# A hybrid decoder block: the last two v tiles made as a pair, round trips issued by two engines, another order at the seams

## The chip, the cores and the metric

The kernel runs on one core of one Trainium2 chip. The metric is the time of one execution on the device in microseconds (us), the median of several runs.

## What is computed

One decoder block on 512 tokens of width 2048 in float32. A modulated RMS norm feeds one input projection; its columns go to two mixers, an RWKV-7 group of 16 heads of 64 (1024 columns each of r, k and v, and small ones for decay, `a` and gate) and a pooling group. Their outputs, 2048 rows, go through an output projection, and a gated MLP with a causal convolution follows.

```python
h = _rmsnorm(x, norm1_g[l]) * (1.0 + sc1) + sh1
p = h @ w_in[l]
y_rwkv = _rwkv7_mixer(p[..., :N_RWKV_COLS], mu_shift[l], w0[l], w2[l], a0[l], a2[l],
                      g2[l], k_k[l], k_a[l], r_k[l], ln_x_w[l], ln_x_b[l])
y_pool = _pool_mixer(p[..., N_RWKV_COLS:], pool_w[l], pool_b[l], pool_scale[l])
mix = jnp.concatenate([y_rwkv, y_pool], axis=-1) @ w_out[l]
x = x + gt1 * mix
h = _rmsnorm(x, norm2_g[l]) * (1.0 + sc2) + sh2
x = x + gt2 * _conv_ffn(h, w_up[l], conv_w[l], conv_b[l], w_down[l])
```

Inside the RWKV mixer every column is first mixed with that of the token before (the token shift), and each head carries a 64x64 state from token to token:

```python
sa = jnp.einsum('bhvk,bhk->bhv', S, a_t)
S = S * w_t[:, :, None, :] + sa[..., None] * b_t[:, :, None, :] + v_t[..., None] * k_t[:, :, None, :]
y = jnp.einsum('bhvk,bhk->bhv', S, r_t)
```

## The kernel before

**Products in three passes.** Each float32 product of a weight tile is made of three matmuls (`mm3`, lines 128 to 130: hi weights by hi activations, hi by lo, lo by hi). `split_weights` loads 128x512 weights into `wraw` (four buffers), ScalarE (ACT) casts the hi part `whi` (L122) and VectorE (DVE) subtracts to get `wlo` (L124). One tile of the input projection, 128 columns by 512 tokens, is 16 k-blocks of 128, that is 48 matmuls of 128x512 and four weight loads. Activations are split in the same way: `split_act` makes `ah` (L151, ACT) and `al` (L152, DVE) from a row of 128 channels.

**Stages.** First the norm and the first tiles of the projection (to about 204 us in the trace), then the mixer stage, four quads of four heads (g = 0 to 3), then the output projection, then the MLP, which takes most of the time. In the mixer stage the small matmuls of the quads, 64x64 or 64x128, stand between tiles of the input projection that make the columns of the next quad: `win_some` makes tiles and writes each, shifted by `shift` (L268 on ACT, L269 on DVE), to DRAM (`spill` to `sp`), and `load_cells` brings them back into the cells R, K and V. For each quad two tiles of k, two of r and two of v are made.

**A quad.** `front` makes the gates: the decay from `sg` (a sigmoid, L423), its running sum, `ep` and the second `sg` (exponentials, L443 and L444), `al` (a sigmoid, L428), and the normaliser `inv` (L451 squares, L452 the sum of them on TensorE, L456 a logarithm, L457 an exponential). Sigmoid, tanh, exponentials and logarithm need tables on ACT, and a load of one shows as ACT_TABLE_LOAD; `preload_act_table_set` (L430) asks for the table with logarithm and exponential early. `rest` does the remainder: `scores` (matmuls L485, masked into `sb` by DVE at L487), tokens in rows by `by_token` (matmuls L497, copied by ACT at L500 into tokTB and tokTV), the same for k (L534, copied at L536 into tokTK), the second scores (L545, masked into `sk` at L547), and a sum over heads (L554).

**The round trips.** A triangular system of 16x16 blocks is solved in another layout. `sb` goes to DRAM in eight transfers (`dn`, L510), comes back as `nl` (L512) once all eight have landed, DVE copies it (L560) and works through 28 small steps (L567, L569) to `xyl`; this goes to DRAM as `dxy` (L573) and comes back into X in eight transfers (L577). PE then multiplies X with the identity (L583) and goes on: L593, the mask into `pm` (L596), L603 and L609, the addition into X (L605), L593 again. All the transfers are issued by SyncE (SP).

**Mixer rows.** The finished rows `rs` of quads 0 to 2 go to DRAM (`mixd`, L706), as do those of the pools (L339). Behind the last quad's front, fourteen rows are read back (`mxl`, L775, in the four `wraw` buffers), split and multiplied by the output weights (`wout`); the last quad's two rows (`last_mix`) are split directly and are used later.

**What sets the order.** The program is written stage by stage; a scheduler places instructions on each engine by their priority (`tc.high_priority`), and each engine then runs its own list in that order. `ada_rest` spreads 96 products for later modulation (`war`, loaded from `ada` at L382, DVE at L383) over spots behind given instructions. PSUM buffers for small products (`bt`) are handed on when the reader of an earlier one is done.

Of the kernel before, what the change touches and what calls it, by code (L numbers as in the profile page):

```python
# [18 lines left out]
P = 128  # L19
# [8 lines left out]
NQ = 4  # L28
# [36 lines left out]
def block_kernel(ctx, tc, a, out, stop=None, dbg=None):  # L65
# [121 lines left out]
    if True:  # L187
# [78 lines left out]
        if True:  # L266
# [13 lines left out]
            xwa = ra.tile([P, T], F32, tag="xwa", name="xwa")  # L280
            shift(pf[0], 24, xwa)
            xg = two(cell("X", "xg"))
            RKV = ("R", "K", "V")
            rkv0 = [cell(RKV[i], "rkv"[i]) for i in range(3)]
            for i in range(2):
                shift(pf[1 + i], 25 + i, xg[:, i, :])
            for i, (t, x, m) in enumerate(((0, 0, 0), (1, 0, 8), (2, 0, 16), (0, 1, 1), (1, 1, 9))):
                shift(pf[3 + i], m, two(rkv0[t])[:, x, :])
                if i == 0:
                    S.activation(xwa[0:64, :], xwa[0:64, :], AF.Tanh)  # L290
            ps0ctx.close()
# [4 lines left out]
            def sigmoids():  # L296
                for i in range(2):
                    S.activation(xg[:, i, :], xg[:, i, :], AF.Sigmoid)
                    S.copy(xgh[i], xg[:, i, :])
                V.tensor_tensor(xg1l, xg[:, 0, :], xg1h[:, :].bitcast(F32), op=ALU.subtract)  # L300
                V.tensor_tensor(xg2[64:96, :], xg[64:96, 1, :], xg2[64:96, :].bitcast(F32), op=ALU.subtract)

            sigmoids()

# [100 lines left out]
    def front(g, rkv):  # L405
# [21 lines left out]
        for x in range(2):  # L427
            act = S.activation(two(al)[:, x, :], psal[:, x, :], AF.Sigmoid, bias=c2("a0", x))  # L428
        with tc.issue_after(act.ins):
            act = S.preload_act_table_set("natural_log_exp_and_others")  # L430
# [33 lines left out]
    def rest(g, rkv, fr):  # L464
# [42 lines left out]
        for s in range(2):  # L507
            for i in range(4):
                o = 64 * s + 16 * i
                nc.sync.dma_start(dn[s, i].rearrange("j i t -> i j t"), nts[o : o + 16, :, 0, 16 * i : 16 * i + 16])  # L510
        nl = ra.tile([P, 16, 16], F32, tag="nl", name="nl")
# [62 lines left out]
        for s in range(2):  # L574
            for i in range(4):
                o = 64 * s + 16 * i
                nc.sync.dma_start(rows(X)[o : o + 16, :, 16 * i : 16 * i + 16],  # L577
                                  dxy[o : o + 16].rearrange("j a t -> a j t"))
# [125 lines left out]
        for x in range(2):  # L704
            if g < NQ - 1:
                nc.sync.dma_start(mixd[2 * g + x], two(rs)[:, x, :])  # L706
            else:
                last_mix.append(split_act(NM + x, two(rs)[:, x, :]))

    sp, last_mix = {}, []  # L710

    def win_some(pairs, which):
# [12 lines left out]
    def load_cells(g, names):  # L725
# [6 lines left out]
        return got  # L732

    UNDER = {0: POOLS[0:1], 1: POOLS[1:2], 2: POOLS[2:4]}
    rkv = rkv0
    with hp():
        fr, norm = front(0, rkv)
    for g in range(NQ):
        pairs = (2 * g + 2, 2 * g + 3)
# [8 lines left out]
        if g < NQ - 1:  # L748
            win_some(pairs, (0, 2))
            with tc.high_priority(offset=50000):  # L750
# [6 lines left out]
        with hp():  # L757
            next(quad, None)
            if g < NQ - 1:
                rkv = [r, k] + load_cells(g + 1, (2,))  # L760
        if g < NQ - 1:
            ada_rest(24 * g, 24 * g + 24)
# [7 lines left out]

    M = []

    def load_mix(i):
        t = wp.tile([P, WC], F32, tag="wraw", name="mxl", bufs=4)
        nc.sync.dma_start(t, mixd[MIX_ORDER[i]])  # L775
        M.append(split_act(i, t))

    for i in range(NM):
        load_mix(i)
    part = []  # L780
# [499 lines left out]
```

## Time and profile before

| what | value |
|---|---|
| median of 3 runs | 2308.88 us (2304.35 to 2310.61) |
| the profiled execution | 2309.01 us, span 2307.2 us |
| TensorE busy | 2197.2 us, 95% |
| VectorE busy | 1509.7 us, 65% |
| ScalarE busy | 926.7 us, 40% |
| mean granted TensorE clock | 0.985 of full speed |

The span is what the profile covers, from the first to the last instruction; the time of the execution has 1.8 us more around it. PE is TensorE's matmuls, DVE VectorE, ACT ScalarE, POOL GpSimd and SP SyncE. A line such as L497 is a line of the kernel, shown above. Where a row has brackets, they give the idle time of the engine just ahead of it and what ended this.

### The profile page before, as it was taken

The numbers are of one execution on the slowest core, as the hardware profiler recorded it, in microseconds if no ns is written. First come the engines' busy times: TensorE is split into PE (matmuls) and PEld (weight loads), VectorE is DVE, ScalarE is ACT, GpSimd is POOL, SyncE is SP. The second block draws the span as 40 slices with busy tenths as digits, with TensorE's granted clock in tenths as the row PEclk, the third lists the DMA queues.
The fourth block names the chain that finished last, engine by engine and source line by source line (L and its number), as shares of the span: only waits on it lengthen the run. The fifth ranks groups of instructions, "written<-read, shape, count | busy, mean of one in ns | idle before, by whom it ended". The sixth has DMA issues, their size and how long they took to land.

```text
span 2307.2 us, 41832 instructions
## 1 busy us (share of the span) xinstructions
PE 2197.2 (95%) x16306; PEld 1874.6 (81%) x16306; DVE 1509.7 (65%) x2536; ACT 926.7 (40%) x1551; POOL 408.0 (18%) x390
## 2 busy tenths in 40 slices
PE   7999898889889999999999999999999999999997
PEld 5786666576667799799999999999999788888886
DVE  7896777686866569866665666656666445464457
ACT  4335242433523355534444444444444333343333
POOL 0000000000000016644334343433432000000000
PEclk9999999999999999999999999999999999999999
DMA  9885656566665575433333333333333766666555
GB/s 355 296 316 164 182 189 193 179 224 200 199 220 173 186 236 172 127 115 119 110 112 117 119 115 111 118 110 109 121 114 118 244 191 211 194 195 202 166 160 179
DMA packets 198041, 401.41 MB, mean 174 GB/s; under 512 B 37585, under 2 KB 50641, under 8 KB 193617
## 3 DMA queue, kind: packets, MB, share of 16 engines
q1 hardware_dynamic: 197842, 398.73, 54.0%
q8 instruction: 128, 2.10, 0.4%
q14 instruction: 71, 0.58, 0.1%
HBM read 364.56 MB, written 34.09 MB: 173 GB/s over the span
## 4 chain that ended last, share of the span: by engine, by line
PE 54%; DMA 1%; DVE 1%; ACT 0%; issue 0%; SPq 0%; DVEq 0%; ACTq 0%
PE b L128 18%; PE b L129 18%; PE b L130 18%; DMA wraw<-wdn 1%; DVE x L1102 0%; DMA ald<-actd 0%; DMA x<-x2d 0%; DVE wlo L124 0%; ACT whi L122 0%; DVE x L831 0%; DVE al L152 0%; PE b L178 0%; ACT ah L151 0%; DVE acc L827 0%; DVE sl L997 0%
## 5 line engine op out<-in xcount | busy, mean ns | idle before, releaser
L122 ACT CAST whi<-wraw 128x512 fp32r<-128x512 f32 (+1 forms) x594 | 361.4, 610 | 847.2 <-DMA wraw<-wup 263.0
L124 DVE TENSOR_TENSOR wlo<-wraw,whi 128x512 fp32r<-128x512 f32 (+1 forms) x578 | 407.3, 708 | 292.3 <-ACT whi L122 285.2
L128 PE MATMUL b<-ah,whi 128*128 128x512 f32 (+1 forms) x980 | 350.0, 357 | 8.1 <-ACT whi L122 7.1
L130 PE MATMUL b<-ah,wlo 128*128 128x512 f32 (+1 forms) x980 | 349.3, 357 | 3.5 <-DVE wlo L124 3.2
L129 PE MATMUL b<-al,whi 128*128 128x512 f32 (+1 forms) x980 | 348.3, 355 | 0.0
L130 PE MATMUL b<-hh,wlo 128*128 128x512 f32 (+1 forms) x640 | 236.6, 370 | 5.2 <-DVE wlo L124 5.2
L128 PE MATMUL b<-hh,whi 128*128 128x512 f32 (+1 forms) x640 | 237.1, 371 | 0.3 <-ACT whi L122 0.3
L129 PE MATMUL b<-hl,whi 128*128 128x512 f32 (+1 forms) x640 | 236.6, 370 | 0.0
L128 PEld LDWEIGHTS b<-ah,whi 128*128 128x128 f32 x980 | 185.8, 190 | 36.6 <-ACT whi L122 10.9
L130 PEld LDWEIGHTS b<-ah,wlo 128*128 128x128 f32 x980 | 185.7, 189 | 32.9 <-DVE wlo L124 6.1
L129 PEld LDWEIGHTS b<-al,whi 128*128 128x128 f32 x980 | 186.0, 190 | 25.7
L997 DVE TENSOR_TENSOR pl<-raw,ph 128x768 fp32r<-128x768 f32 x104 | 102.0, 980 | 154.0 <-ACT ph L996 154.0
L128 PE MATMUL mm<-ah,whi 128*128 128x512 f32 x444 | 183.2, 413 | 6.1 <-ACT whi L122 6.0
L130 PE MATMUL mm<-ah,wlo 128*128 128x512 f32 x444 | 181.0, 408 | 4.4 <-DVE wlo L124 4.4
L129 PE MATMUL mm<-al,whi 128*128 128x512 f32 x444 | 184.0, 414 | 0.0
L985 POOL TENSOR_TENSOR sums<-sums,raw 128x256 f32<-128x256 f32 x104 | 107.2, 1030 | 420.7 <-DVE sl L997 414.8
L130 PE MATMUL b<-tk,sl 128*128 128x256 f32 x624 | 176.7, 283 | 0.5 <-DVE sl L997 0.5
L129 PE MATMUL b<-tk,sh 128*128 128x256 f32 x624 | 176.6, 283 | 0.0
L128 PE MATMUL b<-tk,sh 128*128 128x256 f32 x624 | 176.0, 282 | 0.0
L996 ACT CAST ph<-raw 128x768 fp32r<-128x768 f32 x104 | 86.4, 830 | 167.7 <-PE b L129 160.5
L984 POOL TENSOR_TENSOR sums<-raw 128x512 f32<-128x512 f32 x104 | 136.8, 1315 | 63.4 <-DMA raw<-wups 33.5
L130 PEld LDWEIGHTS b<-hh,wlo 128*128 128x128 f32 x640 | 120.6, 188 | 28.6 <-DVE wlo L124 7.6
(277 smaller groups left out, 4694.4 us busy)
## 6 DMA issues: line engine op xcount, KB each, us to landing
raw<-wups SPq DMA_DIRECT2D x104, 512.0 KB, 3.5
war<-ada SPq DMA_DIRECT2D x96, 512.0 KB, 4.5
wraw<-wdn SPq DMA_DIRECT2D x192, 256.0 KB, 3.2
wraw<-wup SPq DMA_DIRECT2D x160, 256.0 KB, 3.6
wa<-ada SPq DMA_DIRECT2D x32, 1024.0 KB, 7.4
wraw<-win SPq DMA_DIRECT2D x108, 256.0 KB, 4.1
ald<-actd SPq DMA_DIRECT2D x88, 256.0 KB, 2.7
wraw<-wout SPq DMA_DIRECT2D x78, 256.0 KB, 4.0
```

Of the source, the lines that this page charges most:

```text
L122: mark[0] = S.copy(hi[:, 0:w], raw[:, 0:w]).ins
L124: mark[1] = eng.tensor_tensor(lo[:, 0:w], raw[:, 0:w], hi[:, 0:w].bitcast(F32), op=ALU.subtract).ins
L128: PE.matmul(ps, wh, xh, start=start, stop=False)
L129: PE.matmul(ps, wh, xl, start=False, stop=False)
L130: return PE.matmul(ps, wl, xh, start=False, stop=stop)
L984: G.tensor_tensor(sa, raw[:, 1:3, :], raw[:, 0:1, :].to_broadcast([P, 2, W2]), op=ALU.add)
L985: G.tensor_tensor(sb2[:, 0, :], sa[:, 0, :], raw[:, 2, :], op=ALU.add)
L996: act = S.copy(hi[:, sl, :], t)
L997: dve = V.tensor_tensor(lo[:, sl, :], t, hi[:, sl, :].bitcast(F32), op=ALU.subtract)
```

## The change

It has five parts. (1) The shifts of the first tiles get a priority of their own; the sigmoids of xg are called in the first quad's `front`, ahead of the table preload, instead of behind the shifts, and their casts and low parts (`split_gates`) behind that front. (2) Of the eight transfers of `dn` and of X in each quad, those of the second half of the tokens (s = 1) are issued by ACT, the others by SP as before. (3) For the fourth quad's columns `win_some` makes only k and r; the two v tiles are made together by `win_two`, a weight load of one and of the other in turn, and shifted from PSUM straight into the cell V, with no trip through DRAM. (4) Twelve mixer rows are loaded and split right behind those two tiles in the program. (5) The third quad's rows are split directly from `rs`, like those of the fourth, and take places 12 and 13 of the activations.

```diff
--- before.py
+++ after.py
@@ -278,16 +278,17 @@
                 return t[:, 0 : 2 * T].rearrange("p (x t) -> p x t", x=2)
 
             xwa = ra.tile([P, T], F32, tag="xwa", name="xwa")
-            shift(pf[0], 24, xwa)
-            xg = two(cell("X", "xg"))
-            RKV = ("R", "K", "V")
-            rkv0 = [cell(RKV[i], "rkv"[i]) for i in range(3)]
-            for i in range(2):
-                shift(pf[1 + i], 25 + i, xg[:, i, :])
-            for i, (t, x, m) in enumerate(((0, 0, 0), (1, 0, 8), (2, 0, 16), (0, 1, 1), (1, 1, 9))):
-                shift(pf[3 + i], m, two(rkv0[t])[:, x, :])
-                if i == 0:
-                    S.activation(xwa[0:64, :], xwa[0:64, :], AF.Tanh)
+            with tc.high_priority(offset=200000):
+                shift(pf[0], 24, xwa)
+                xg = two(cell("X", "xg"))
+                RKV = ("R", "K", "V")
+                rkv0 = [cell(RKV[i], "rkv"[i]) for i in range(3)]
+                for i in range(2):
+                    shift(pf[1 + i], 25 + i, xg[:, i, :])
+                for i, (t, x, m) in enumerate(((0, 0, 0), (1, 0, 8), (2, 0, 16), (0, 1, 1), (1, 1, 9))):
+                    shift(pf[3 + i], m, two(rkv0[t])[:, x, :])
+                    if i == 0:
+                        S.activation(xwa[0:64, :], xwa[0:64, :], AF.Tanh)
             ps0ctx.close()
             xgh = [ra.tile([P, T], F32R, tag=f"xgh{i}", name=f"xgh{i}") for i in range(2)]
             xg1h, xg2 = xgh
@@ -295,12 +296,15 @@
 
             def sigmoids():
                 for i in range(2):
-                    S.activation(xg[:, i, :], xg[:, i, :], AF.Sigmoid)
+                    act = S.activation(xg[:, i, :], xg[:, i, :], AF.Sigmoid)
+                return act
+
+            def split_gates():
+                for i in range(2):
                     S.copy(xgh[i], xg[:, i, :])
                 V.tensor_tensor(xg1l, xg[:, 0, :], xg1h[:, :].bitcast(F32), op=ALU.subtract)
                 V.tensor_tensor(xg2[64:96, :], xg[64:96, 1, :], xg2[64:96, :].bitcast(F32), op=ALU.subtract)
 
-            sigmoids()
 
     def load_pw(gi):
         pw = [ra.tile([P, 2, P], F32, tag="lg", name="pw"), ra.tile([P, 3, P], F32, tag="gw", name="pw")[:, 0:2, :]]
@@ -426,6 +430,8 @@
         al = cell("AL", "al")
         for x in range(2):
             act = S.activation(two(al)[:, x, :], psal[:, x, :], AF.Sigmoid, bias=c2("a0", x))
+        if g == 0:
+            act = sigmoids()
         with tc.issue_after(act.ins):
             act = S.preload_act_table_set("natural_log_exp_and_others")
         n = 2 * NK * (C + 1)
@@ -507,7 +513,7 @@
         for s in range(2):
             for i in range(4):
                 o = 64 * s + 16 * i
-                nc.sync.dma_start(dn[s, i].rearrange("j i t -> i j t"), nts[o : o + 16, :, 0, 16 * i : 16 * i + 16])
+                (nc.sync, nc.scalar)[s].dma_start(dn[s, i].rearrange("j i t -> i j t"), nts[o : o + 16, :, 0, 16 * i : 16 * i + 16])
         nl = ra.tile([P, 16, 16], F32, tag="nl", name="nl")
         nc.sync.dma_start(nl, dn[:, :, :, :, :].rearrange("s i j a t -> (s i j) a t"))
         X = cell("X", "X")
@@ -574,7 +580,7 @@
         for s in range(2):
             for i in range(4):
                 o = 64 * s + 16 * i
-                nc.sync.dma_start(rows(X)[o : o + 16, :, 16 * i : 16 * i + 16],
+                (nc.sync, nc.scalar)[s].dma_start(rows(X)[o : o + 16, :, 16 * i : 16 * i + 16],
                                   dxy[o : o + 16].rearrange("j a t -> a j t"))
         yield
         ps = batch()
@@ -702,12 +708,20 @@
             PE.matmul(pg[:, x, :], gw[:, 1, :], xg2, start=False, stop=True)
         V.tensor_mul(flat(rs), flat(rs), wide(pg))
         for x in range(2):
-            if g < NQ - 1:
+            if g < NQ - 2:
                 nc.sync.dma_start(mixd[2 * g + x], two(rs)[:, x, :])
             else:
-                last_mix.append(split_act(NM + x, two(rs)[:, x, :]))
+                (M if g == NQ - 2 else last_mix).append(split_act(2 * g + x + NM - 2 * NQ + 2, two(rs)[:, x, :]))
 
     sp, last_mix = {}, []
+
+    def win_two(pairs, i):
+        pss = [mmtile() for _ in pairs]
+        for k0 in range(0, KT, WC // P):
+            k1 = k0 + WC // P
+            for p, ps in zip(pairs, pss):
+                project(ps, a["win1"][3 + 3 * p + i - 8, :, k0 * P : k1 * P], H[k0:k1], start=k0 == 0, stop=k1 == KT)
+        return pss
 
     def win_some(pairs, which):
         for p, i in [(p, i) for p in pairs for i in which]:
@@ -731,10 +745,18 @@
             got.append(t)
         return got
 
+    M = []
+
+    def load_mix(i):
+        t = wp.tile([P, WC], F32, tag="wraw", name="mxl", bufs=4)
+        nc.sync.dma_start(t, mixd[MIX_ORDER[i]])
+        M.append(split_act(i, t))
+
     UNDER = {0: POOLS[0:1], 1: POOLS[1:2], 2: POOLS[2:4]}
     rkv = rkv0
     with hp():
         fr, norm = front(0, rkv)
+    split_gates()
     for g in range(NQ):
         pairs = (2 * g + 2, 2 * g + 3)
         with hp():
@@ -746,7 +768,12 @@
             for gi in UNDER.get(g, ()):
                 pool(gi)
         if g < NQ - 1:
-            win_some(pairs, (0, 2))
+            win_some(pairs, (0, 2) if g < NQ - 2 else (0,))
+            if g == NQ - 2:
+                pss = win_two(pairs, 2)
+                with tc.high_priority(offset=50000):
+                    for i in range(NM - 2):
+                        load_mix(i)
             with tc.high_priority(offset=50000):
                 r, k = load_cells(g + 1, (0, 1))
         with hp():
@@ -756,8 +783,13 @@
                 fr, norm = front(g + 1, (r, k, None))
         with hp():
             next(quad, None)
-            if g < NQ - 1:
+            if g < NQ - 2:
                 rkv = [r, k] + load_cells(g + 1, (2,))
+            elif g == NQ - 2:
+                v = cell("V", "v")
+                for x in range(2):
+                    shift(pss[x], 16 + pairs[x], two(v)[:, x, :])
+                rkv = [r, k, v]
         if g < NQ - 1:
             ada_rest(24 * g, 24 * g + 24)
         if g == 2:
@@ -768,15 +800,6 @@
 
 
 
-    M = []
-
-    def load_mix(i):
-        t = wp.tile([P, WC], F32, tag="wraw", name="mxl", bufs=4)
-        nc.sync.dma_start(t, mixd[MIX_ORDER[i]])
-        M.append(split_act(i, t))
-
-    for i in range(NM):
-        load_mix(i)
     part = []
     for f in range(NW):
         if f % 2 == 0:
```

How the instructions stand on the engines, by the order of the two programs. New lines have other numbers than old ones: 516 is the old 510, 518 the old 512, 553 the old 547, 566 to 575 the old 560 to 569, 752 the old 775, and of front's activations 427, 432, 449, 450, 457, 462 and 463 are the old 423, 428, 443, 444, 451, 456 and 457.

ACT at the first quad's gates, before: xwa, xg, r and k are the shifted first columns.

```order
L451 ACTIVATE inv<-k,vec 128x512
L268 ACTIVATE k<-pf_990,drv 128x512
L298 ACT_TABLE_LOAD
L298 ACTIVATE xg<-xg 128x512 x2
L451 ACTIVATE inv<-k,vec 128x512
L299 CAST xgh_1770<-xg 128x512
L299 CAST xgh_1771<-xg 128x512
L122 CAST whi<-wraw 128x512 x2
L423 ACTIVATE sg<-bt,vec 128x8x64 x2
L428 ACTIVATE al<-bt,vec 128x512 x2
L430 ACT_TABLE_LOAD
L443 ACTIVATE ep<-sg 128x1040
```

Here one table load serves xg, sg and al, and the preload of L430 stands behind al. ACT at the same place, after:

```order
L299 ACT_TABLE_LOAD
L299 ACTIVATE xg<-xg 128x512 x2
L436 ACT_TABLE_LOAD
L457 ACTIVATE inv<-k,vec 128x512 x2
L122 CAST whi<-wraw 128x512 x2
L304 CAST xgh_1770<-xg 128x512
L304 CAST xgh_1771<-xg 128x512
L427 ACT_TABLE_LOAD
L427 ACTIVATE sg<-bt,vec 128x8x64 x2
L432 ACTIVATE al<-bt,vec 128x512 x2
L122 CAST whi<-wraw 128x512
L449 ACT_TABLE_LOAD
```

The load of L430 (now L436) has moved from behind al to right behind the xg sigmoids, and loads stand ahead of sg, ep, the logarithm and the last two exponentials.

DVE in quad 0 around the return of `nl`, before:

```order
L383 SCALAR_TENSOR_TENSOR war,modq<-war,cq 128x1024 x2
L547 TENSOR_TENSOR sk<-bt,masks 128x2x512 x2
L324 TENSOR_TENSOR sw<-sw 128x2x525
L556 TENSOR_TENSOR v<-bt,v 128x1024
L560 COPY xyl<-nl 128x256
L324 TENSOR_TENSOR sw<-sw 128x2x521
L561 MEMSET xyl 128x16
L567 TENSOR_TENSOR prod<-xyl,nl 128x14
```

Here both sk products stand ahead of the copy from nl (L560). DVE at the same place, after:

```order
L387 SCALAR_TENSOR_TENSOR war,modq<-war,cq 128x1024 x3
L124 TENSOR_TENSOR wlo<-wraw,whi 128x512
L566 COPY xyl<-nl 128x256
L567 MEMSET xyl 128x16
L573 TENSOR_TENSOR prod<-xyl,nl 128x14
L575 TENSOR_TENSOR xyl<-xyl,prod 128x14
L573 TENSOR_TENSOR prod<-xyl,nl 128x26
L553 TENSOR_TENSOR sk<-bt,masks 128x2x512
L575 TENSOR_TENSOR xyl<-xyl,prod 128x2x13
```

The copy from nl and the first steps of the triangular system have moved ahead of both sk products; in quad 1 the copy stands between the two, in quad 2 ahead of both.

SP at the seam to the fourth quad, before: each mixd with its own number is another mixer row.

```order
L718 DMA sp_2_5514<-spill 128x512
L775 DMA mxl<-mixd_104 128x512
L775 DMA mxl<-mixd_105 128x512
L775 DMA mxl<-mixd_106 128x512
L730 DMA v<-sp_2_5514 128x512
L510 DMA dn_6235<-sb 16x16x16 x8
L775 DMA mxl<-mixd_101 128x512
L775 DMA mxl<-mixd_102 128x512
L775 DMA mxl<-mixd_97 128x512
L512 DMA nl<-dn_6235 128x256
L775 DMA mxl<-mixd_98 128x512
```

Here dn follows ten of the mixer rows, and nl follows thirteen. SP at the same place, after:

```order
L516 DMA dn_6305<-sb 16x16x16 x4
L752 DMA mxl<-mixd_93 128x512
L752 DMA mxl<-mixd_94 128x512
L386 DMA war<-ada 128x1024
L518 DMA nl<-dn_6305 128x256
L752 DMA mxl<-mixd_95 128x512
L752 DMA mxl<-mixd_96 128x512
L752 DMA mxl<-mixd_107 128x512
L752 DMA mxl<-mixd_108 128x512
L386 DMA war<-ada 128x1024
L752 DMA mxl<-mixd_103 128x512
L752 DMA mxl<-mixd_104 128x512
```

Ten mixer rows were issued ahead of the fourth quad's dn; now all twelve stand behind it, and ten of them behind nl. On PE, L485, the first L497 and L534 of the fourth quad now stand inside the pair of v tiles, with 39 of its 96 matmuls ahead and 57 behind; the second L497, L545, L554 and the first output tile follow the pair. L583 stands in one piece in each quad, after 18 matmuls of its tile in quad 0 (before, 23 and 14 more around its two pieces).

## Rows read from the trace of the kernel before

**Rows 1.** The page, part 1: busy time, share of the span and instructions by engine.

```profile
PE 2197.2 (95%) x16306; PEld 1874.6 (81%) x16306; DVE 1509.7 (65%) x2536; ACT 926.7 (40%) x1551; POOL 408.0 (18%) x390
```

**Rows 2.** Stretches: length, busy by engine (x instructions), PEclk, DMA share, GB/s.

```profile
200.00:240.00 40.00, 33.55 (x382) 23.83 (x384) 33.76 (x44) 26.43 (x38) 0.95 (x1) 0.91 0.35 104
...
591.50:641.90 50.40, 36.83 (x426) 28.93 (x424) 42.61 (x68) 23.51 (x37) 0.00 (x0) 0.87 0.74 225
```

**Rows 3.** Waits of PE, 180 to 740 us: total, times, longest, all in us.

```profile
PE bt L593 <- DVE X L605: 8.8, 2, 5.4
...
PE mm L128 <- ACT whi L122: 6.0, 1, 6.0
...
PE bt L583 <- DMA X<-dxy: 2.3, 2, 1.4
```

**Rows 4.** Timeline of ACT, first quad's gates: start, length, instruction, [idle before <-releaser].

```profile
205.72 0.68 ACT L268 ACTIVATE k<-pf,drv 128x512 f32<-128x512 f32 x1
206.42 1.28 ACT L298 ACT_TABLE_LOAD   x1
207.72 1.15 ACT L298 ACTIVATE xg<-xg 128x512 f32<-128x512 f32 x2
...
211.45 1.25 ACT L423 ACTIVATE sg<-bt,vec 128x512 f32<-128x512 f32 x2
...
216.71 1.07 ACT L443 ACTIVATE ep<-sg 128x1040 f32<-128x1040 f32 x1 [1.55 <-DVE sg L437]
...
222.19 1.06 ACT L457 ACTIVATE inv<-inv 128x1024 f32<-128x1024 f32 x1
```

**Rows 5.** Timeline of PE at the same gates, then at L554 of quads 0 and 2.

```profile
212.76 2.93 PE L452 MATMUL bt<-inv,cmat 128*128 128x512 f32 x3 [3.57 <-ACT sg L423]
...
243.01 1.98 PE L554 MATMUL bt<-al,cmat 128*128 128x512 f32 x4 [1.09 <-DVE sk L547]
...
500.38 1.12 PE L554 MATMUL bt<-al,cmat 128*128 128x512 f32 x2 [0.47 <-DVE sk L547]
```

**Rows 6.** SP's DMA issues of the first round trip, quads 0 and 2.

```profile
237.12 5.53 SPq L510 DMA_DIRECT2D dn<-sb  x8
...
244.16 0.33 SPq L512 DMA_DIRECT2D nl<-dn  x1
...
492.03 4.85 SPq L510 DMA_DIRECT2D dn<-sb  x8
...
498.32 0.33 SPq L512 DMA_DIRECT2D nl<-dn  x1
```

**Rows 7.** Timeline of DVE: normaliser, sk and nl of quad 0, nl of quad 2, a war of quad 1.

```profile
224.07 1.41 DVE L459 SCALAR_TENSOR_TENSOR inv<-k,vec,inv 128x512 f32<-128x512 f32 x2
...
241.74 2.35 DVE L547 TENSOR_TENSOR sk<-bt,masks 128x1024 f32<-128x1024 f32 x2
...
249.08 0.29 DVE L560 COPY xyl<-nl 128x256 f32<-128x256 f32 x1 [2.70 <-DMA nl<-dn]
...
504.05 0.29 DVE L560 COPY xyl<-nl 128x256 f32<-128x256 f32 x1 [0.30 <-DMA nl<-dn]
...
407.38 1.23 DVE L383 SCALAR_TENSOR_TENSOR war<-war,cq 128x1024 f32<-128x1024 f32 x1 [6.23 <-DMA war<-ada]
```

**Rows 8.** Seam to the fourth quad: PE, SP's issues, then line L775's landing times.

```profile
616.85 0.39 PE L128 MATMUL mm<-ah,whi 128*128 128x512 f32 x1
617.08 0.39 PE L129 MATMUL mm<-al,whi 128*128 128x512 f32 x1
...
618.30 1.98 PE L485 MATMUL bt<-ar,inv 64*64 64x128 f32 x64
...
641.87 0.80 PE L128 MATMUL mm<-ah,whi 128*128 128x512 f32 x1 [6.02 <-ACT whi L122]
...
625.36 4.78 SPq L510 DMA_DIRECT2D dn<-sb  x8
...
DMA to landing us min/median/max: 2.7/3.7/5.1
```

## The prediction, made before the changed kernel ran

> **What bounds the kernel now.** I read the page's busy times first: TensorE (PE) is busy 95% of the span [rows 1], so a change pays only where PE stands idle or runs at a low clock, and costs wherever it makes PE stand longer. The total of matmuls stays the same here (no product is added or dropped). The view by stretches of 40 us shows where PE is not full: in the mixer stage, 200 to about 735 us; the first such stretch has 33.55 us busy of 40 at a mean granted clock of 0.91 [rows 2]. Then the view of waits names who was late there [rows 3]: the addition into X (L605), twice, the weights of the first output tile (once, 6.0 us), the return of X (L583). Last I read the timelines of the engines at the places that the change touches.
>
> The clock needs a price. A mean of 0.91 over 40 us is 3.6 us of full-speed time gone if PE had work throughout [rows 2], that is one stretch of some 7 us at 1.2 instead of 2.4 GHz. It fell there around the 3.57 us idle before L452 [rows 5]. Such a stretch overlaps the idle time, so I take 1.7 us (half) for each one that comes or goes, with 0 and 3.6 as its ends.
>
> One profiled execution took 2309.01 us (span 2307.2 and 1.8 around it), 0.1 above the median of the runs, 2308.88. I add the sum to 2309.0.
>
> **1. The head, where the first quad's gates are made.** The xg sigmoids move into `front`, ahead of the table preload in program order, and the order of ACT shows what comes of it: the preload (L430) stands between the xg sigmoids and those of sg and al, so the sigmoid table is loaded again for sg, and three loads follow for ep, Ln and the two last exps. Four loads more at 1.28 us [rows 4] are 5.1 us of ACT. Two lie ahead of sg: 2.6 us later. The one for ep hides in the 1.55 us that ep waited for DVE [rows 4]. The other two, 2.6 us, lie between ep and the last exp; before, this piece lasted from 216.71 to 223.25, 6.5 us for four activations of about 1.05, and the rest was casts and waits that stand elsewhere now, so it stays near 6.5. The last exp ends some 2.5 us later. DVE picked it up 0.8 us late before (224.07 for an end at 223.25 [rows 4, 7]), so 1.7 us reach DVE, and one *war* product of 1.2 us leaves the chain to L487 while one wlo of 0.6 enters. Net **+1.1 us** at sb. The wait at L452 itself, 3.57 us, gets 2.6 longer and has seven matmuls more in front of it (1.6 us). Bounds: 0.5, if DVE regains more, and 2.5, if nothing does.
>
> The Trainium skill (ScalarE: Activation LUTs, What ACT_TABLE_LOAD costs) counts 2.66 us for a switch, since a drain of 1.38 us goes with the load. The rows speak against it here: the activation ahead ended at 206.40, the load ran from 206.42 and the next began at 207.72 [rows 4]. By the page four loads would be 10.6 us and the head about +6, the whole near 2312.
>
> **2. The first round trip (sb, dn, nl, xyl).** Eight issues in a row on SP take 5.53 and 4.85 us in quads 0 and 2, and nl is issued 1.5 us after the last [rows 6]. With four on SP and four on ACT, nl is issued at T+4.3 and T+3.9 instead of T+7.0 and T+6.3 (T: first dn issue). Its transfer takes 4.9 and 5.7 us (issued 244.16 and 498.32, DVE started 249.08 and 504.05 [rows 6, 7]), so it lands at T+9.2 and T+9.6 instead of T+12. That is 2.4 to 2.7 us gained. ACT's tokTB and tokTK copies stand behind the four issues, but they waited for PE there anyway.
>
> What takes the gain back is DVE's order. The copy from nl (L560) now stands ahead of the sk product (L547) in quads 0 and 2, and DVE works in order. PE's L554 needs the PSUM buffer that the first sk product frees. Before, that product ran at 241.74 and L554 at T+5.9 and T+8.4 [rows 5 to 7]. Now: nl lands at T+9.2, the copy and three or four small steps take about 1.1, sk 1.2, so L554 at T+11.5 (quad 2: T+11.6 with fewer steps ahead). In quad 0 that is 5.6 us later, of which six matmuls (1.4 us) have been put in front; in quad 2 it is 3.2 later, and nothing moved. PE has nothing else in its order. I take **+4.2** (quad 0) and **+3.2** (quad 2); bounds 3 and 6, 1 and 5. In quad 1 the first sk product still stands ahead of the copy: 0. Each idle time of 5 us may bring a low stretch; one of the two is counted, as quad 2 had one there: **+1.7**.
>
> **3. The second round trip (dxy, X) and L583.** Four of eight issues on ACT save about 2.3 us, and xyl starts 2.5 earlier. L583 now comes in one piece and earlier among the matmuls (after 18 of its tile instead of split at 23 and 37). X is some 5 us earlier and PE some 3 later in quad 0, so the 1.4 us there go [rows 3]: **−1.4**; another 0.9 in quad 3: **−0.9**. ACT waits for dxy ahead of two whi casts, which have buffers ahead.
>
> The wait at L605 is not one of the change's own: DVE stood 6.23 us at a *war* product whose load was late, ahead of L605 in quad 1 [rows 7], and PE lost 5.4 of the 8.8 us there [rows 3]. SP issues that load eight places behind X now instead of nine, and SP is free 2 us earlier. Still a *war* stands ahead of L605. I take **−3** for quad 1, 0 for quad 0; bounds −9 and 0 for both.
>
> **4. The seam to the fourth quad.** From the end of the second of the last three weight pairs' tiles (591.5) to the first output matmul (641.87) PE is busy 36.83 of 50.40 us at 0.87 [rows 2]: 13.6 idle. Four gate matmuls of this (0.9 us) lie ahead of the mark E in the new order, so 49.5 us are to be compared. By the new order: 39 matmuls at 0.227 us (616.85 to 617.08 [rows 8]), 8.9, then L485. Before, the dn issue came 7.06 us after L485 began (618.30, 625.36 [rows 8]), with 2.7 in which DVE waited for a spill shift and made an al; now some 3.8, at E+12.8, and PE waits 3.0 for sb. L497 and L534 take 2.2; then 57 matmuls, 12.9 us, to E+29. nl (E+22) and the first al products are hidden by them. What ends last then is the loading of the mixer rows. They are issued behind dn and partly behind nl, so from E+15 on, through four wraw buffers that the last win weights hold too; a load takes 3.7 us median, up to 5.1 [rows 8], and its cast sits in ACT's order between the two v shifts and ahead of tokTB and tokTV. Three rounds of about 5 us put load 9 at E+30 and load 11 at E+34. So tokTV's product waits 2 to 5 us, sk waits for al10 (it stands behind it on DVE), L554 comes at E+36 to E+41 and the first output matmul at E+38 to E+43. Against 49.5: a gain of 6.5 to 11.5; I take **−8**, nearest to the loads' median. If the loads never wait for a buffer it is E+34.5, a gain of 15; if each round takes the 6 us that the late wout tile waited [rows 3], E+46, a gain of 3.5.
>
> **The sum:** 1.1 + 4.2 + 3.2 + 1.7 − 1.4 − 0.9 − 3 − 8 = −3.1, so 2305.9, say 2306. About 0.3% (6.9 us) is what a measurement of this kernel can tell from no change, so this is "within", on the near side of faster.
>
> **Rivals.** *The seam closes.* The mixer loads come as fast as the casts take them, 15 us instead of 8, and the *war* ahead of L605 in quad 1 lands in time, 5 instead of 3: 2306 − 9 = 2297. For it: only twelve rows come from DRAM instead of fourteen, and the DMA engines are not full; against it: their share is 0.74 in this stretch, twice the 0.35 of the first [rows 2].
>
> *The slower one: two queues bring nl no sooner, and DVE stands for it.* If the transfers, not the issues, set the landing, nl stays at T+12 and L554 comes 2.6 us later still in quads 0 and 2: +5.2. Each of these waits would be 7 to 8 us long, twice the 3.57 beside which the clock fell before [rows 5], so I let both bring a whole low stretch, 7.2 instead of 1.7: +5.5; X's wait in quad 0 stays: +1.4. That is 2318. It decides from a landing later than about T+11 on. For it: nl is issued only 1.5 us after the last dn issue, so the early ones had long landed. Against it: that same 1.5 us says that the last issue sets it, and it now comes 2.5 us sooner. The Trainium skill (DMA: Bandwidth & Descriptors, Rules for kernel authors) is on this side as far as bandwidth goes: queues of several engines share the same sixteen DMA engines, and using more only saves issue time. By the rows, issue time is just what is long here.
>
> *The seam does not do what it says.* The loads trail until E+46 and the pair only moves the wait from the first output tile to L497 and L554: 2306 + 4.5 = 2310.
>
> **Chances.** Forecast 0.45 (2302 to 2311), seam closes 0.25 (2297), nl stands in the way 0.20 (2318), seam only moved 0.10 (2310). Faster by over 0.3% (under 2302.0): the second case and a tenth of the first, 0.30. Slower (over 2315.8): the third and a little of the rest, 0.22. Within: 0.48. The range leaves out the extremes of the second and third case: 2292 to 2319.
>
> **What would show it.** Right: four more table loads between 205 and 225 us; PE idle before L554 of 4 to 6 us in quads 0 and 2, released by sk, with DVE standing at the copy from nl; dn issues in two rows of four; no wait of 6 us at the first output tile, but waits at L497, at L554, with ACT waiting for mixer rows. Wrong: L554 without a wait (then nl came by T+6, or the sk product ran first), the first output matmul later than 46 us behind E, or new waits after 735 us, where nothing is moved.

## The result, and the profile after

The changed kernel takes 2326.08 us (median of six runs, 2319.96 to 2327.82), the kernel before 2309.45 beside it: a ratio of 1.0069, 95% interval 1.0056 to 1.0083. It is slower by 16.6 us where 2306 was forecast, and it lies above the range. The profiled execution took 2324.27 us, with a span of 2322.5; the span of before was 2307.2, so there are 15.3 us to find.

Line numbers have moved: L554 of before is L560 now, L547 is L553 (sk), L560 is L566 (the copy from nl), L510 is L516 (dn), L583 is L589, L593 is L599, L605 is L611.

The page's busy line of after answers [rows 1]; PE is busy 6.1 us longer with the same number of matmuls, so it ran slower somewhere:

```profile
PE 2203.3 (95%) x16306; PEld 1875.2 (81%) x16306; DVE 1510.0 (65%) x2536; ACT 929.1 (40%) x1555; POOL 408.6 (18%) x390
```

Where is it? I cut both traces at the first gate matmul of each quad. These are the four stretches of before: from and to, length, busy time of PE, PEld, DVE, ACT and POOL, mean granted clock of PE, DMA share, GB/s.

```profile
204.34:323.42 119.08, 104.50 (x1468) 74.67 (x1471) 87.57 (x161) 45.99 (x79) 0.95 (x1) 0.96 0.55 164
323.42:445.99 122.57, 108.88 (x1506) 77.67 (x1500) 90.37 (x166) 45.27 (x75) 0.95 (x1) 0.97 0.62 197
445.99:579.22 133.23, 122.40 (x1555) 88.01 (x1549) 97.14 (x179) 49.91 (x82) 0.95 (x1) 0.97 0.65 203
579.22:776.55 197.33, 177.54 (x1790) 134.91 (x1783) 128.05 (x229) 70.72 (x120) 0.95 (x1) 0.95 0.60 184
```

The same four of after:

```profile
204.76:333.35 128.59, 104.33 (x1452) 73.02 (x1454) 86.11 (x159) 49.32 (x81) 0.95 (x1) 0.92 0.50 149
333.35:456.69 123.34, 110.42 (x1503) 78.26 (x1498) 91.52 (x167) 45.70 (x76) 0.95 (x1) 0.96 0.61 193
456.69:595.25 138.56, 122.05 (x1546) 86.61 (x1540) 96.80 (x178) 49.02 (x81) 0.95 (x1) 0.95 0.64 194
595.25:791.95 196.70, 182.02 (x1818) 139.18 (x1811) 128.81 (x231) 71.84 (x122) 0.95 (x1) 0.97 0.57 178
```

The lengths alone mislead, since matmuls of the projections move between stretches. Three numbers are to be worked out of each row: the idle time (length less PE's busy time), the price of the low clock (one less the clock, times the length), and what is left, PE's work at full speed. Idle time changed by +9.7, -0.8, +5.7 and -5.1 us, the clock's price by +5.5, +1.2, +2.9 and -4.0, the work by -5.7, +0.3, -3.3 and +8.5 (each to about 1 us, as the clock has two digits). Idle time and clock make 15.1 of the 15.3 us: +15.2 in quad 0, +0.4, +8.6 in quad 2 and -9.1 in quad 3. The last looks just like the gain forecast at the seam; the experiments show that it is something else.

Who was late, by the view of PE's waits of after, 180 to 760 us (total, times, longest), against [rows 3]:

```profile
PE bt L560 <- DVE sk L553: 15.8, 4, 6.2
PE bt L599 <- DVE X L611: 6.4, 2, 5.2
...
PE bt L599 <- issue: 5.7, 3, 3.3
...
PE bt L589 <- DMA X<-dxy: 2.9, 2, 2.7
...
PE mm L128 <- ACT whi L122: 1.3, 2, 0.9
```

The 6.0 us at the first output tile are gone. In their place L560, the old L554, waits 15.8 us for sk. The timelines of quad 0 show how, to be laid beside [rows 5 to 7]; SP's issues of after:

```profile
240.57 1.99 SPq L516 DMA_DIRECT2D dn<-sb  x4
...
244.73 0.33 SPq L518 DMA_DIRECT2D nl<-dn  x1
```

DVE at the return of nl, after:

```profile
250.22 0.29 DVE L566 COPY xyl<-nl 128x256 f32<-128x256 f32 x1 [3.20 <-DMA nl<-dn]
...
251.07 1.22 DVE L553 TENSOR_TENSOR sk<-bt,masks 128x1024 f32<-128x1024 f32 x1
```

PE at the same place, after:

```profile
246.06 1.10 PE L551 MATMUL bt<-ar,sg 64*64 64x128 f32 x32 [0.31 <-ACT tokTV L506]
252.34 3.78 PE L560 MATMUL bt<-al,cmat 128*128 128x512 f32 x4 [5.18 <-DVE sk L553]
```

PE had made sk's product by 247.2, and DVE could have multiplied it by the masks at once. DVE stood 3.20 us at the copy from nl instead, which is ahead in its list, and PE stood behind DVE. And then PE was slow as well: these four matmuls took 3.78 us where they took 1.98 before [rows 5]. The view by stretches, with the same columns as above, has the clock; after, behind the wait:

```profile
252.34:262.00 9.66, 9.66 (x26) 6.41 (x27) 8.29 (x16) 0.82 (x2) 0.00 (x0) 0.70 0.01 2
```

and before, around L554:

```profile
243.00:253.00 10.00, 9.05 (x35) 6.55 (x36) 7.30 (x12) 2.45 (x4) 0.00 (x0) 1.00 0.54 146
```

So an idle time of 5.18 us was followed by 9.66 us in which PE never stopped and was granted 0.70 of its clock on average: 2.9 us on top. In quad 2 of after, SP's issues first (ACT's four had begun at 505.30):

```profile
506.74 3.58 SPq L516 DMA_DIRECT2D dn<-sb  x4
...
511.71 0.33 SPq L518 DMA_DIRECT2D nl<-dn  x1
```

then DVE,

```profile
517.91 0.29 DVE L566 COPY xyl<-nl 128x256 f32<-128x256 f32 x1 [9.75 <-DMA nl<-dn]
518.33 1.22 DVE L553 TENSOR_TENSOR sk<-bt,masks 128x1024 f32<-128x1024 f32 x1
```

and PE:

```profile
519.60 2.07 PE L560 MATMUL bt<-al,cmat 128*128 128x512 f32 x2 [6.18 <-DVE sk L553]
```

PE in quad 1 of after, where nothing was expected:

```profile
386.60 1.13 PE L560 MATMUL bt<-al,cmat 128*128 128x512 f32 x2 [2.49 <-DVE sk L553]
```

There the first sk product had run at 379.93, ahead of the copy (383.32), but the second came behind it, at 385.33.

ACT in the head of after, against [rows 4]:

```profile
213.41 1.28 ACT L427 ACT_TABLE_LOAD   x1
...
219.95 1.28 ACT L449 ACT_TABLE_LOAD   x1 [2.33 <-DVE sg L443]
221.25 1.07 ACT L449 ACTIVATE ep<-sg 128x1040 f32<-128x1040 f32 x1
222.34 1.28 ACT L462 ACT_TABLE_LOAD   x1
...
224.71 1.28 ACT L450 ACT_TABLE_LOAD   x1
...
226.98 1.04 ACT L463 ACTIVATE inv<-inv 128x1024 f32<-128x1024 f32 x1
```

The four added loads are there. But the one for ep begins when sg has come (219.95), not while ACT waits for it. The last exp ends at 228.02 instead of 223.25.

At the seam, against [rows 8], PE of after waits for the shifted v tile and for sk:

```profile
648.35 0.45 PE L503 MATMUL bt<-cmat,v 64*64 64x64 f32 x2 [4.34 <-DVE v L269]
...
656.52 2.83 PE L560 MATMUL bt<-al,cmat 128*128 128x512 f32 x4 [1.94 <-DVE sk L553]
```

This last wait is not behind the copy from nl, which ran at 641.37, 14 us ahead of the sk product (655.25).

### The profile page after: what moved, and what is told of

Its sections match the earlier page's. It is cut to its first block, busy times and chain, and to the rows that moved or that the text cites. A ratio compares the mean times of both kernels' runs of the same rounds, so it can differ in the third digit from the quotient of the medians.

```text
span 2322.5 us, 41818 instructions
## 1 busy us (share of the span) xinstructions
PE 2203.3 (95%) x16306; PEld 1875.2 (81%) x16306; DVE 1510.0 (65%) x2536; ACT 929.1 (40%) x1555; POOL 408.6 (18%) x390
## 4 chain that ended last, share of the span: by engine, by line
PE 54%; DMA 1%; DVE 1%; ACT 0%; issue 0%; SPq 0%; DVEq 0%; ACTq 0%
PE b L130 18%; PE b L128 18%; PE b L129 18%; DMA wraw<-wdn 1%; DVE x L1125 0%; DMA x<-x2d 0%; DMA ald<-actd 0%; DVE wlo L124 0%; ACT whi L122 0%; DVE al L152 0%; ACT ah L151 0%; PE b L178 0%; DVE sl L1020 0%; DVE x L854 0%; PE b L165 0%
## 5 line engine op out<-in xcount | busy, mean ns | idle before, releaser
L128 PEld LDWEIGHTS b<-ah,whi 128*128 128x128 f32 x980 | 185.8, 190 | 37.3 <-ACT whi L122 11.5
```

The lines of the kernel that those rows point to most:

```text
L128: PE.matmul(ps, wh, xh, start=start, stop=False)
```

## The experiments

Theory A: the loss is DVE's order at the copy from nl, and splitting dn over two engines is what made the scheduler choose that order. Rival B: the two queues themselves cost (issue, landing, ACT's time). Rival C: head and seam make up the difference. All ratios are to the kernel before, in brackets the 95% interval. Under each text that says what was expected stands what was measured.

**The order alone, and each part undone in the changed kernel.** The pin lets the copy from nl start only behind the second sk product, in quads 0 to 2:

```
+        skdve = dve
...
-        V.tensor_copy(xyl[:, 1, :, :], nl)
+        back = V.tensor_copy(xyl[:, 1, :, :], nl)
+        if g < NQ - 1:
+            in_step(back, skdve.ins)
```

> The changed kernel with one order pinned: in quads 0 to 2 DVE's copy from nl stands behind both sk products again; the two issuing engines stay. Theory A (the order on DVE is what costs): PE's waits for sk at L554, 5.2, 2.5 and 6.2 us in quads 0 to 2, go, and so do two or three of the low-clock stretches behind them; 2326 minus 14 of idle and some 5 of clock, so 2305 to 2311. Theory B (the issues by two engines delay the transfers, and the order only shows it): the waits move to X and to the war products ahead of L605, and 2318 to 2326 stays.

Measured: 1.0029 (1.0011 to 1.0048), 2310.36 us.

Trips undone is at both places

```
-                (nc.sync, nc.scalar)[s].dma_start(
+                nc.sync.dma_start(
```

> The changed kernel with all dn and X transfers issued by SP again; DVE's order of sk and nl goes back by itself. Theories A and B both: quads 0 to 2 lose the 18.9 us that the ledger of the two traces shows there, so 2305 to 2309 (head +3.5, seam -7 remain). If the loss came from the seam or the head: 2318 or more.

Measured: 1.0012 (1.0001 to 1.0024). Head undone, in short:

```
+            sigmoids()
...
-        if g == 0:
-            act = sigmoids()
...
-    split_gates()
```

> The changed kernel with the head as before (shifts, sigmoids and their casts; 14 table loads instead of 18). By the two traces the first quad's scores start 3.5 us later in the changed kernel at the same work. Theory A and B: 2322 to 2323 (3.5 us less). If a later wait takes the head start up (nl or X bound in quad 0), 2325 to 2326.

Measured: 1.0049 (1.0035 to 1.0062). Seam undone, in short:

```
-            win_some(pairs, (0, 2) if g < NQ - 2 else (0,))
-            if g == NQ - 2:
-                pss = win_two(pairs, 2)
...
+            win_some(pairs, (0, 2))
...
+    for i in range(NM):
+        load_mix(i)
```

> The changed kernel with the seam to the fourth quad as before (v tiles made one by one through DRAM, fourteen mixer rows read back). The ledger says that the new seam is worth 7 us: 2331 to 2335. If the seam only moved its waits, 2324 to 2328.

Measured: 1.0077 (1.0063 to 1.0091). Against 1.0069 of the whole, the trips make 0.57%, the head 0.20%, the seam nothing that shows. The pin gives back 0.40% with both trips kept, and its waits of PE at sk (here L561) show why:

```profile
PE bt L561 <- DVE sk L553: 2.8, 3, 1.1
```

**Parts alone, on the kernel before.** The edits are the hunks above, put in instead of taken out; with the trips in the last quad alone, `[s]` reads `[s if g == NQ - 1 else 0]`.

> The kernel before with the new head alone (18 table loads). Theory A1 (the head costs what the first quad's start shows): 3.5 us more than before, ratio 1.0010 to 1.0020. Theory A2 (undoing it in the changed kernel gave 0.2% back, so it costs more than its own start): 5 to 8 us, 1.0021 to 1.0035. If quad 0 takes it up in its later waits: within 0.1% of before.

Measured: 1.0018 (1.0007 to 1.0028).

> The kernel before with both round trips issued by two engines and nothing pinned: DVE's copy from nl then stands ahead of both sk products in quads 0 and 2 and between them in quad 1, as in the changed kernel. Theory A: the order adds what it added in the changed kernel (1.0069 against 1.0029), so 1.0020 (trips with sk first) plus 0.0040: 1.0050 to 1.0070. If the order hurts only together with the new head or seam: 1.0010 to 1.0030.

Measured: 1.0071 (1.0054 to 1.0089): the trips alone are as slow as the whole change.

> The kernel before with the new seam alone. By subtraction (trips undone 1.0012, head alone 1.0018): 0.9985 to 1.0000, a gain of 0 to 3 us. By the prediction's sum (8 us): 0.9965.

Measured: 1.0002 (0.9988 to 1.0015).

> The kernel before with the round trips issued by two engines in the fourth quad alone; old head, old seam, order in quads 0 to 2 as before. Theory A: only the fourth quad changes, 6 to 8 us of its 27.6 lost go: ratio 0.9965 to 0.9975. If the fourth quad's gain came from work that was pushed back from quads 0 to 2 (13 more matmuls of the tiles stood behind it there): 0.9990 to 1.0005.

Measured: 0.9994 (0.9985 to 1.0003). In the last quad the copy from nl now stands between the two sk products (634.86, with 632.90 and 636.76; behind both before), but L554 waited no longer than before for the first, 0.4 us, and the trips cost nothing.

> The kernel before with both round trips issued by two engines and the copy from nl held behind both sk products in quads 0 to 2; old head, old seam. If the trips help the fourth quad by themselves (theory A: with the seam undone its idle and low-clock time was 19.0 us against 27.6 before, so the new seam was not what took it down): 2306 minus 8, plus some 3 in quads 1 and 2, ratio 0.9970 to 0.9990. If that gain needs the new seam: 1.0000 to 1.0020.

Measured: 1.002 (1.0006 to 1.0034). Against 1.0071 without the pin, it is worth 0.51% here.

> The changed kernel with the old head and the copy from nl held behind both sk products in quads 0 to 2: trips and new seam are what is left. If the three causes add up: 1.0029 (sk first, with the new head) minus 0.0015 to 0.0030 for the head, so 1.0000 to 1.0015. If the new seam is worth the 7 us of the prediction: 0.9970.

Measured: 1.0000 (0.9988 to 1.0012): without the head, and with the pin, the rest of the change is worth nothing either way. Order (0.40%) and head (0.29%) make up the 0.69% of the whole.

**The two trips apart.** Only the line of dn, then the same with the pin, then only the line of X:

```
-                nc.sync.dma_start(dn[s, i]
+                (nc.sync, nc.scalar)[s].dma_start(dn[s, i]
```

> The kernel before with only the first round trip (dn) issued by two engines and nothing pinned: the copy from nl stands ahead of sk in quad 0 and between the sk products in quads 1 and 2. With sk first the same kernel gave 0.9996, so the difference is the order alone. Theory A with a wait at L554 in quad 0 alone (its price there 5 to 6 us and a low stretch): 1.0015 to 1.0040. If the order were no cause: 0.9990 to 1.0005.

Measured: 1.0071 (1.0058 to 1.0084).

> The kernel before with only the first round trip (dn) issued by two engines, the copy from nl behind both sk products in quads 0 to 2. Both trips so: 1.0020. If the second trip (X, for which ACT waits until dxy has landed, ahead of casts) is what costs: 0.9990 to 1.0005. If the first one costs: 1.0015 to 1.0030.

Measured: 0.9996 (0.9984 to 1.0008). These two have the same DMAs on the same queues and differ in the pin and in the order that follows from it: 0.75%, some 17 us. Waits of PE of dn alone:

```profile
PE bt L554 <- DVE sk L547: 14.5, 4, 4.8
PE bt L593 <- DVE X L605: 12.7, 4, 5.9
```

and of dn with the pin:

```profile
PE bt L596 <- DVE X L608: 1.7, 2, 1.2
PE bt L555 <- DVE sk L547: 1.3, 1, 1.3
```

The stretch in which quad 0's nl comes back, of dn alone (columns as above):

```profile
240.00:280.00 40.00, 33.27 (x242) 23.88 (x241) 29.51 (x68) 11.48 (x17) 0.00 (x0) 0.91 0.53 146
```

With the pin:

```profile
240.00:280.00 40.00, 36.72 (x308) 27.37 (x301) 32.91 (x75) 12.50 (x19) 0.00 (x0) 1.00 0.63 170
```

DVE with the pin makes both sk products, and then waits for nl at no one's cost:

```profile
246.34 1.23 DVE L547 TENSOR_TENSOR sk<-bt,masks 128x1024 f32<-128x1024 f32 x1 [0.19 <-PE bt L545]
250.33 0.29 DVE L561 COPY xyl<-nl 128x256 f32<-128x256 f32 x1 [2.76 <-DMA nl<-dn]
```

One reserve: with the copy pinned the scheduler also set other things otherwise (the first product of X stands later), so the 17 us are not those of two instructions swapped. The waits at sk fell by 13.2 us, but those at the addition into X by 11.0 as well. And in quad 2 of dn alone it isn't the copy that holds sk up: DVE stood for a late *war* load ahead of the first product, and PE waited 4.83 us.

```profile
506.39 1.23 DVE L383 SCALAR_TENSOR_TENSOR war<-war,cq 128x1024 f32<-128x1024 f32 x1 [6.62 <-DMA war<-ada]
```

In the changed kernel the three waits of quads 0 to 2 are behind the copy, as the timelines above show, and there the pin gives back 0.40%; how much of the 0.75% is the copy's alone isn't shown.

> The kernel before with only the second round trip (X) issued by two engines. If this trip is what made 1.0020 of 0.9996 when both trips ran with sk first: 1.0015 to 1.0030. If the two trips only cost together (or the difference was the runs): 0.9990 to 1.0008.

Measured: 1.0017 (1.0005 to 1.0028). So B holds for the second trip, on a small scale: X by two engines is a loss.

**The war products behind L605.** `spots` lists the DVE instructions behind which a *war* product may stand. Two of each quad, one of the four behind xyl and the one behind the first pm, move from ahead of the addition into X to behind it:

```
-        spots[g] += [dve.ins] * 4
+        spots[g] += [dve.ins] * 3
...
-            spots[g].append(dve.ins)
...
-                V.tensor_add(flat(X), flat(X), wide(ps))
+                dve = V.tensor_add(flat(X), flat(X), wide(ps))
+                spots[g] += [dve.ins] * 2
+            else:
+                spots[g].append(dve.ins)
```

> The kernel before with nothing but the war products given places behind the addition into X. With the new seam this gave 0.9958 and the seam alone 1.0002: if they add up, 0.9950 to 0.9965. If the gain needed the seam: 0.9985 to 1.0000.

Measured: 0.9974 (0.9964 to 0.9984).

> The kernel before with the new seam, and one change of the order that the traces point to: one of the four war products behind xyl, and the one behind the first pm, are given a place behind the addition into X (L605), so that no late war load stands ahead of it. PE waited 8.8 us for that addition before, with low-clock stretches behind. If that wait goes: 0.9950 to 0.9970, faster than both kernels. If the late load only stops DVE one product further on: 0.9985 to 1.0000.

Measured: 0.9958 (0.9943 to 0.9973), 2296.56 us: the lowest ratio of all, ahead of both kernels, though its interval overlaps those of 0.9967 and 0.9974 here. With the seam alone PE waited at the addition into X:

```profile
PE bt L594 <- DVE X L606: 13.6, 3, 6.0
...
PE mm L128 <- ACT whi L122: 1.8, 1, 1.8
```

With the *war* moved no wait for the addition into X is left in the stretch; the longest names the next DVE product behind it:

```profile
PE bt L612 <- DVE pm L597: 7.4, 2, 4.4
```

> The kernel before with the first trip by two engines, sk first and the war products later; old head, old seam, X by SP. If the parts add up: 0.9996 + 0.9958 - 1.0002, so 0.9945 to 0.9960, the fastest of all. If X or the seam then becomes the later one: 0.9960 to 0.9975.

Measured: 0.9967 (0.9955 to 0.998), dn with the pin and the later *war*.

> The kernel before with the first round trip by two engines and sk first, the new seam and the war products later; old head, X by SP. By the parts (0.9967 for the same without the seam, seam 1.0002, war with seam 0.9958): 0.9945 to 0.9970, faster than both kernels. If seam and first trip collide on SP and ACT in the fourth quad: 0.9970 to 0.9990.

Measured: 0.9979 (0.9965 to 0.9994), the two before it together: no sum, the gains do not add.

> The kernel before with the second round trip (X) issued by two engines and the war products given places behind the addition into X. X by two engines alone gave 1.0017, the war products alone 0.9974. If what X by two engines costs is a late war product ahead of L605 (PE gets there earlier and stands at L593 and L609): 0.9965 to 0.9980, as without the split. If the split costs by itself (ACT waiting for dxy, or a shared ring): 0.9985 to 1.0000.

Measured: 1.0009 (0.9997 to 1.0021). X by two engines costs 0.35% here too, beside 0.9974 without it. It isn't the place of the *war* products that makes it lose. The waits of PE say where it loses: at the first L593 of quads 1 and 2 PE paused part of the way through its 64 matmuls, with no releaser named. Of this run, and of the *war* alone (there in quad 0):

```profile
PE bt L593 <- issue: 9.4, 2, 5.0
...
PE bt L593 <- issue: 2.4, 1, 2.4
```

These 7.0 us more are of the size of the 0.35% (8 us), in one execution of each. With X alone the line had 5.8, before 0.3. What PE waits for there stays open.

## Why the prediction was wrong

**The head (+1.1).** Right in sign, too small. Three pairs of runs give 0.18% (alone), 0.20% (undone) and 0.29% (with the pin, 1.0029 to 1.0000), each to 0.1 or 0.2%: 4 to 7 us, above the bound of 2.5. The step that failed is "the one for ep hides in the 1.55 us that ep waited for DVE": the load came behind the wait, and the last exp ended 4.8 us later, not 2.5. The first product of quad 0's mixer, L485 before and L491 now, began at 231.75 and 235.26, so 3.5 us reached PE. How the rest of the 4 to 7 us arises isn't shown. The price of a load held, 1.28 us each, the next activation 0.01 to 0.02 us behind it. The Trainium skill's 2.66 us for a switch (ScalarE: Activation LUTs, What ACT_TABLE_LOAD costs) is not what these rows show, though the head of some +6 that I estimated from it came nearer the measured one than mine (by the sum, +6 makes 2311 and not the 2312 that stands there).

**L554 behind the copy from nl (+4.2, 0, +3.2, clock +1.7).** The mechanism is right, and it is the cause of the loss; the terms were too small. By T, the first dn issue, quad 0 went as worked out: nl issued at T+4.2, copied at T+9.7 and L554 at T+11.8, for 4.3, 9.2 and 11.5; the wait grew by 4.1 for 4.2. Three steps failed. (1) Quad 2: nl was copied at T+12.6, not T+9.6 (T is 505.30, ACT's first dn). SP, with a load of v ahead of them (506.32), began its four issues 1.4 us after ACT and took 3.58 us for them, so that its last ended at T+5.0, where eight in a row had ended at T+4.85 [rows 6]; nl then took 6.2 us instead of 5.7. L554 came at T+14.3, and the wait grew by 5.7, not 3.2. (2) Quad 1 was put at 0 and waited 2.49: the first sk product stood ahead of the copy, but the second stood behind it. The waits at this line rose by 13.8 us in all (2.0 to 15.8), 12.3 of them in quads 0 to 2; the 1.94 of quad 3 belong to the seam, where DVE has sk behind the mixer rows. (3) One low stretch of 1.7 us was counted; the clock's price rose by 5.6 over the four stretches, head and seam included, and 2.9 of it is the stretch behind quad 0's wait alone. The rival that "two queues bring nl no sooner, and DVE stands for it" is what happened in quad 2, and its 2318 was nearer. What I set against it, that the last issue "now comes 2.5 us sooner", is what quad 2 contradicts.

**The second trip (-1.4, -0.9).** Wrong in sign: X's wait in quad 0 grew to 2.71 us, and X by two engines alone costs 0.17%. The step that failed is "X is some 5 us earlier": X's issues came at T+37.5, before at T+31.6. What I had not priced is the way there in the new order. SP's issues of quad 0, before:

```profile
266.72 0.33 SPq L573 DMA_DIRECT2D dxy<-xyl  x1
...
268.76 5.36 SPq L577 DMA_DIRECT2D X<-dxy  x8
```

and after:

```profile
269.92 0.45 SPq L386 DMA_DIRECT2D war<-ada  x1
...
271.40 0.33 SPq L579 DMA_DIRECT2D dxy<-xyl  x1
...
278.05 3.79 SPq L583 DMA_DIRECT2D X<-dxy  x4
```

From the copy of nl to the issue of dxy 21.2 us passed, 17.6 before: the two sk products, 2.4 us, stand among the small steps now. X's issues came 6.6 us behind that of dxy, 2.0 before, with a *war* load 1.5 us ahead of dxy; that the load made it slow is likely, not shown. And the four issues took 3.79 us.

**The wait at L605 (-3).** In quad 1 it went, all 5.4 us of it: the *war* product ahead of the addition waited 0.82 us for its load, not 6.23 [rows 7]:

```profile
419.06 1.23 DVE L387 SCALAR_TENSOR_TENSOR war<-war,cq 128x1024 f32<-128x1024 f32 x1 [0.82 <-DMA war<-ada]
```

But in quad 0 it grew from 3.35 to 5.15, and quad 3 has a new one of 1.23, so that 6.4 us are left of 8.8: -2.4. What no term has are the pauses with no releaser named at the first L599 of quads 1 and 2, 2.1 and 3.3 us, as in the runs with X by two engines above. A cure that held was to take the *war* products from ahead of the addition, 0.26% by itself; the wait for pm behind it grew from 2.2 to 8.2 us in that run, so some of the wait only moved.

**The seam (-8).** The place went nearly as read: the first output matmul came some 43 us behind the mark E (614.9 to 658.4), at the late end of "E+38 to E+43", for 49.5 before. The 6-us wait at the first output tile went, and waits came for v (4.3 at L503) and at L560 (1.94). But no time came of it: alone it is 1.0002. The step that failed is taking a stretch shorter by 8 us for a kernel shorter by 8 us. By itself the seam lost the 4.2 us that it saved at whi (6.0 to 1.8) at the addition into X (8.8 to 13.6, with a new wait of 4.0 in the fourth quad). And the 9 us that quad 3 gained in the whole change are there without the seam's edit. Fourth stretch of the changed kernel with the seam undone:

```profile
591.63:788.44 196.81, 181.51 (x1819) 137.47 (x1811) 129.85 (x231) 72.24 (x122) 0.95 (x1) 0.97 0.60 189
```

Its idle time and low clock are 15.3 and 5.9 us, those of the whole change 14.7 and 5.9, those of before 19.8 and 9.9. What both have in common is more work in that stretch, 7.9 and 8.5 us at full speed more than before, and in the whole change 9.0 us less in quads 0 and 2: matmuls that no longer stood in the gaps there fill those here. With the trips in the last quad only, the stretch's work was that of before (180.88 us busy less 13.8 for the clock, 167.1; before 167.7); its idle time fell by 3.4 us, the clock took 3.9 more, and it gained nothing. So the gain in quad 3 goes with the loss ahead of it, by these three runs; which matmul fills which gap isn't shown.

## What to carry to other kernels

Here DVE worked off its list in order, standing 3.20 and 9.75 us at the copy with a product for PE behind it. So when a round trip is made shorter, look at where the scheduler now puts the instruction that waits for its return: ahead of work that another engine needs, it can cost more than the trip saves. A pinned order gave back most of it here, and the same goes for a filler whose load comes late, as the *war* products did. When an activation is moved, count the table loads it causes and where they stand; one that begins behind a wait is not hidden by it. A stretch that became shorter is no gain until the neighbours that gave it their work, or took its wait, have been read too.

## What the runs showed of the hardware

Four dn issues on SP beside four on ACT took 1.99 us in quad 0 and 3.58 us in quad 2, where eight on SP alone had taken 5.53 and 4.85 [rows 6]: halving them saved 3.5 and 1.3 us, and in quad 2 the last one ended no sooner. After an idle time of 5.18 us, PE ran without a pause for 9.66 us at a mean granted clock of 0.70, where the kernel before, with 1.09 us idle at the same place, had 1.00; the levels are 1.2 and 2.4 GHz, so some six of those microseconds were at the lower one. The idle time just ahead doesn't settle it alone: with the trips in the last quad only, the same four matmuls of the fourth quad took 3.78 us behind 0.39 us idle, and the granted clock was 0.62 over 5.8 us from there.
